# A bidirectional encoder layer: x read once, its squares summed by column, and a second weight group on normalized rows with fused pairs

## The chip, the cores and the metric

One core of one Trainium2 chip runs the kernel. The metric is the device time of one execution in microseconds (us), the median of several runs. Engines are named as in the profile: PE (TensorE, the matmuls), PEld (its weight loads), DVE (VectorE), ACT (ScalarE), POOL (GpSimd, here only the issue of some transfers), SP (the queue that issues most transfers). PSUM is where matmuls accumulate; SBUF holds the tiles that engines read and write.

## The reference

256 positions of width 4096, one layer, everything in float32. The attention itself (three dilated windows, combined) is left out below; it isn't touched.

```python
def rms_norm(x, g, eps=NORM_EPS):
    y = x * lax.rsqrt(jnp.mean(x * x, axis=-1, keepdims=True) + eps) * g

xn = rms_norm(x, norm_g[l])
h = jnp.einsum('bsd,de->bse', xn, w_in[l])            # (256, 4096) x (4096, 14336)
c_val, c_glu, c_gate, q, k, v, a_gate = jnp.split(h, split_pts, axis=-1)
conv_out = conformer_conv(c_val, c_glu, ...) * silu(c_gate)   # c_val * sigmoid(c_glu), conv of 31 taps, LayerNorm, silu
q, k = rms_norm(q, ...), rms_norm(k, ...)
attn_out = longnet_mixture(q, k, v, rel_bias) * silu(a_gate)
x = x + jnp.einsum('bse,ed->bsd', concatenate([conv_out, attn_out]), w_out[l])
```

## The kernel before

**Groups and pairs.** The 18432 columns of both projections are cut into 18 groups of 1024 columns: 14 for `w_in`, 4 for `w_out`. A group has two halves `e` of 512 columns and, with the two halves `s` of 128 positions, four PSUM banks. The 4096 rows of a weight group are 32 row tiles `k` of 128, taken as 16 pairs of 1 MB. Each value goes to PE as two parts, `h` (a cast to the matmul's type) and `l` (what the cast lost), and a product is three matmuls of 128x512: h by h, l by h, h by l. A pair is so 24 matmuls (`plain`, L1253 and L1255); in the first group 12 for each row tile `k` (`products`, L953 to L956).

**Fused pairs.** `fused` (L1112 to L1114, L1224, L1226) does a pair in seven products, 21 matmuls, of sums of weight blocks and sums of row blocks. Its weight sums are made by DVE and ACT when the pair comes (`split_fused`, L1074 to L1096), its row sums once for each pair number (`block_sums`, in `xsum`). `FUSED[g]` lists the pairs of group g that are done so: none in the first two groups, then 5, 7, 7, 7, 7, 6, later none, and 4, 7, 7, 7 in the output groups: 64.

**The order.** It is written out by the program, engine by engine, in one pass. `Stream.step` splits weights as soon as one of four slots (`W_SLOTS`) is free: a cast on ACT (L1026, L1051) and a subtraction on DVE (L1027, L1057), and then asks SP for the pair three places on. Between products, `pump` hands out other work to DVE and ACT by a count of nanoseconds (`left`) that each matmul refills (`credit`). `split_gens` is a list of steps that turn a row tile into normalized parts `nh`, `nl`.

**The first two groups.** The first group multiplies with `xh`, `xl` (x times g, made by `split_x` three row tiles ahead). Meanwhile x is loaded a second time by rows (`load_x`, eight 512 KB pieces), ACT squares it with a running sum (`square_x`, L277), and near the end `finish_rstd` makes 1/rms in a small 128x2 tile and sends it through DRAM to have it as a row. The second group multiplies with `xh`, `xl` again and applies 1/rms when its PSUM banks are read; in it x is loaded a third time by columns, and `split_xn` makes `nh`, `nl` for the groups after it.

Of the kernel before, what the change touches and what calls it, by code (L numbers as in the profile page):

```python
# [11 lines left out]
F32 = mybir.dt.float32  # L12
# [5 lines left out]
P = 128  # L18
# [25 lines left out]
C4 = 16  # L44
XN_LOAD = {1 + (5 * c + 1) // 2: c for c in range(8)}
XN_SQUARE = {n + 5 + s: (c, s) for n, c in XN_LOAD.items() for s in range(2)}
EVAC_TABLE = {"conv": AF.Sigmoid, "agv": AF.Silu, "gate": AF.Silu}
# [17 lines left out]
SUMS = max(FUSED)  # L65
FUSED += [range(4)] + 3 * [range(7)]
# [66 lines left out]
def layer_kernel(  # L133
# [37 lines left out]
    def rsqrt(src, shape, mul, eps, name, wait=True):  # L171

        n = int(np.prod(shape[1:]))
        tag, bufs = ("rs_small", 6) if n <= 32 else ("rs_big", 5)
        v = sb.tile(shape, F32, tag=tag, bufs=bufs, name=name + "v")
        r = sb.tile(shape, F32, tag=tag, bufs=bufs, name=name + "r")
        t = sb.tile(shape, F32, tag=tag, bufs=bufs, name=name + "t")
# [78 lines left out]

    ss = const.tile([P, 2, 8], F32, name="ss")
    xT, x_chunks = {}, {}

    def load_xT(k0, n, queue):  # L260

        t = t4(f"xT{k0}")
        queue.dma_start(
            t[:, :n, :].rearrange("p a b -> p (a b)"),
            x_cols[:, KT + S * k0 : KT + S * (k0 + n)],
        )
        for i in range(n):
            xT[k0 + i] = t[:, i, :]

    def load_x(c):  # L270
        t = t4(f"x{c}").rearrange("p a b -> p (a b)").rearrange("p (s d) -> p s d", s=2)
        nc.sync.dma_start(t, xs[:, :, 512 * c : 512 * c + 512])
        x_chunks[c] = t

    def square_x(c, s):
        junk = t2(f"junk{c}_{s}")
        nc.scalar.activation(  # L277
            junk, x_chunks[c][:, s, :], AF.Square, accum_out=ss[:, s, c : c + 1]
        )

    def split_x(k):
        h, l = new_split(k, "x")
        src = xT.pop(k)
        nc.scalar.activation(h, src, AF.Copy, scale=g_cols[:, k : k + 1])
        nc.vector.scalar_tensor_tensor(
            l, src, g_cols[:, k : k + 1], h.bitcast(F32), op0=ALU.mult, op1=ALU.subtract
        )
        xh[k], xl[k] = h, l
        spend(480, 500)

    def split_xn(k):

        src = xT[k]
        nc.vector.scalar_tensor_tensor(
            src, src, g_cols[:, k : k + 1], state["rstd_row"], op0=ALU.mult, op1=ALU.mult
        )
# [5 lines left out]
        yield 0, 400  # L302
        nc.vector.tensor_sub(l, src, h.bitcast(F32))
        xnh[k], xnl[k] = h, l
        yield 415
        if k % 2 and k // 2 in SUMS:
            yield from block_sums(
                k // 2, src_of=xT, parts=(xnh, xnl), out=xsum, name="xs",
                small=k // 2 in SUMS[5:],
            )  # L310

    split_gens = deque()

    def split_more():

        for gen in list(split_gens)[:4]:
            cost = next(gen, None)
            if cost is None:
                split_gens.remove(gen)
            else:  # L320
                spend(*(cost if isinstance(cost, tuple) else (cost,)))

    def block_sums(j, src_of, parts, out, name, small=False):
# [31 lines left out]

    def finish_rstd():
        tot = const.tile([P, 2], F32, name="sstot")
        nc.vector.reduce_sum(tot, ss, axis=AX.X)
        r = yield from rsqrt(tot, [P, 2], 1.0 / D, NORM_EPS, "rx", wait=False)
        keep = const.tile([P, 2], F32, name="rstd")  # L360
        nc.vector.tensor_copy(keep, r)
        state["rstd"] = [keep[:, s : s + 1] for s in range(2)]
        flat = tc.dram_tile([2, P], F32, name="rstd_dram")
        for s in range(2):
            nc.sync.dma_start(flat[s, :].rearrange("(p o) -> p o", o=1), keep[:, s : s + 1])
        row = const.tile([P, S], F32, name="rstd_row")
        nc.sync.dma_start(
            row, bass.AP(tensor=flat.tensor, offset=flat.offset, ap=[[0, P], [1, S]])
        )
        state["rstd_row"] = row  # L370

# [215 lines left out]
    def ln_gen():  # L587
        while 3 not in conv_done:
            yield
        pm = yield from channel_mean([cT[cb] for cb in range(4)], "mu")  # L590
        mu = sb.tile([P, S], F32, tag="rs_big", bufs=5, name="mu")
        nc.scalar.copy(mu, pm[:, :S])
# [246 lines left out]
    def more_rows():  # L839
        if split_gens:  # L840
            split_more()
        else:
            pump(PRODUCT)
# [39 lines left out]
    def evacuate_sum(g, e, s, acc):  # L883
# [3 lines left out]
        fused = (g, e) in more_tiles  # L887
        if not fused and s == 0 and (g, e) != (1, 1):
            plain_tiles[(g, e)] = half_tile(g, e)
        tile_, pair = (more_tiles if fused else plain_tiles).get((g, e)) or plain_tiles[(g, 0)]  # L890
        t = pair[:, s, :]
        if fused:
            nc.vector.tensor_add(t, t, acc)
            spend(690)
            if fn != AF.Copy:
                nc.scalar.activation(t, t, fn)
                spend(0, 620)
        elif g == 1 and e == 1:
            tile_, first = plain_tiles[(g, 0)]
            t = first[:, s, :]  # L900
            nc.vector.scalar_tensor_tensor(
                t, acc, state["rstd"][s], t, op0=ALU.mult, op1=ALU.mult
            )
            spend(745)
        else:
            scale = state["rstd"][s] if g == 1 else 1.0
            nc.scalar.activation(t, acc, fn, scale=scale)
            spend(0, 620)
# [56 lines left out]
    class Stream:  # L965
# [159 lines left out]
        def group(self, g):  # L1125
# [16 lines left out]
            for slot, j in enumerate(ORDERS[g]):  # L1142
# [5 lines left out]
                self.more = W_MORE if firsts and slot + 2 >= firsts[0] else 0  # L1148
                if g == 1 and slot % 2 == 0 and slot < n_pairs - 2:
                    load_xT(2 * slot + 4, 4, nc.sync)  # L1150
                if slot == 7 and into:
# [26 lines left out]
                if slot < n_pairs - 1:  # L1178
                    self.plain(u, j, rows, one, slot == 0)
                    if g == 1:  # L1180
                        split_gens.extend(split_xn(k) for k in (2 * j, 2 * j + 1))
                    continue
# [17 lines left out]
                if g == 1:  # L1200
                    split_gens.extend(split_xn(k) for k in (2 * j, 2 * j + 1))

# [113 lines left out]
    xT[0] = first_x[:, KT:]  # L1316
    load_pair(0, (0, 512, 1024, 2048), between=lambda: load_xT(1, 1, nc.sync))
    load_xT(2, 2, nc.sync)
    load_pair(1, (0, 1024, 2048))
    load_xT(4, 4, nc.sync)  # L1320
    load_pair(2)
    load_xT(8, 4, nc.sync)
    nc.scalar.copy(warm, ones[:, 0:1])
# [7 lines left out]
    stream.step()  # L1331
    rstd_steps = None
    for g in range(n_in):
        if g > 0:
            stream.group(g)
            continue
        for k in range(KT):
            n = g * KT + k
            if n == 0:
# [3 lines left out]
                for m in (2, 3):  # L1343
                    split_x(m)
                    stream.step()
                rstd_steps = finish_rstd()
            else:
# [11 lines left out]
                else:  # L1359
                    products(n, 1, 0)  # L1360
                    products(n, 1, 1)
            if n % 4 == 0 and 12 + n < KT:
                load_xT(12 + n, 4, nc.sync)
            if n == KT - 4:
                load_xT(0, 4, nc.sync)
            if n in XN_LOAD:
                load_x(XN_LOAD[n])
            if n in XN_SQUARE:
                square_x(*XN_SQUARE[n])
            if k == KT - 3 and groups[g][0] in EVAC_TABLE:  # L1370
                nc.scalar.activation(warm, ones[:, 0:1], EVAC_TABLE[groups[g][0]])
            if 26 <= n <= 28:
                next(rstd_steps)
            elif n == 29:
                list(rstd_steps)
            pump()
# [66 lines left out]
```

## Time and profile before

| what | value |
|---|---|
| runs of the kernel before | 1565.12, 1565.15, 1566.41 us, median 1565.15 us |
| the profiled execution | 1565.9 us, its span 1564.1 us |
| mean granted TensorE clock in it | 1.000 |
| PE busy | 1559.1 us, 6874 matmul records |
| DVE, ACT busy | 1335.1 us, 971.0 us |
| moved by the DMA engines | 357.22 MB, mean 228 GB/s |

The span goes from the first to the last instruction; the execution's time lies 1.8 us around it. Matmuls are pipelined: a record of 128x512 lasts 390 ns, while the next one starts 227 ns after it. One float32 matmul that is not split into parts shows as two records.

### The profile page before, as it was taken

What the parts mean: (1) busy time and instruction counts of PE and PEld (TensorE: products, weight loads), DVE (VectorE), ACT (ScalarE), POOL (GpSimd) and SP (SyncE); (2) the same over time, 40 slices, a digit from 0 to 9 for tenths busy, and PEclk for the clock granted to TensorE, in tenths of its full rate; (3) what the DMA queues carried; (4) which work ended last, traced back from release to release, by engine and by line L of the source; (5) the groups of instructions that cost most, each with busy time, mean ns of one, the idle gap of its engine ahead of it and who ended that gap; (6) DMA issues with size and microseconds to landing.
All of it is one profiled execution on the core that took longest, in us unless ns stands there. A gap on an engine that the chain in (4) does not pass through costs nothing.

```text
span 1564.1 us, 18620 instructions
## 1 busy us (share of the span) xinstructions
PE 1559.1 (100%) x6874; PEld 1290.6 (83%) x6874; DVE 1335.1 (85%) x1495; ACT 971.0 (62%) x1503; POOL 98.9 (6%) x184
## 2 busy tenths in 40 slices
PE   9999999999999999999999999999999999999999
PEld 7888888888888888888888888888888888888887
DVE  5658898999999999898798898789575888999988
ACT  6755555565556566667776786776557754555453
POOL 0000000000000000001130022021010400000000
PEclk9999999999999999999999999999999999999999
DMA  9768565655656555659686488567674965666663
GB/s 373 293 220 298 189 224 206 226 191 201 233 212 228 199 207 213 216 190 284 219 279 216 174 256 269 194 206 272 220 239 161 282 233 201 239 240 242 223 248 122
DMA packets 64523, 357.22 MB, mean 228 GB/s; under 512 B 9104, under 2 KB 11920, under 8 KB 27824
## 3 DMA queue, kind: packets, MB, share of 16 engines
q1 hardware_dynamic: 54096, 326.38, 59.1%
q0 software_dynamic: 10048, 29.37, 6.3%
q8 instruction: 54, 0.88, 0.2%
q10 hardware_dynamic: 288, 0.28, 0.1%
q14 instruction: 37, 0.30, 0.1%
HBM read 337.09 MB, written 18.91 MB: 228 GB/s over the span
## 4 chain that ended last, share of the span: by engine, by line
PE 99%; DMA 0%; DVE 0%; SPq 0%; ACT 0%; DVEq 0%; issue 0%
PE c L1253 44%; PE c L1255 22%; PE m L1224 6%; PE c L1269 4%; PE m L1226 3%; PE c L1271 2%; PE c L1114 2%; PE c L1112 2%; PE c L1224 2%; PE c L1113 2%; PE acc L956 2%; PE acc L953 2%; PE acc L954 2%; PE m L1114 1%; PE c L1226 1%; PE m L1113 1%
## 5 line engine op out<-in xcount | busy, mean ns | idle before, releaser
L1057 DVE TENSOR_TENSOR wl<-raw,wh 128x2048 fp32r<-128x2048 f32 x208 | 475.7, 2289 | 150.2 <-ACT wh L1051 140.9
L1051 ACT CAST wh<-raw 128x1024 fp32r<-128x1024 f32 x416 | 414.9, 1048 | 222.1 <-PE c L1255 134.7
L1253 PE MATMUL c<-wh,nh 128*128 128x512 f32 x1128 | 439.6, 390 | 0.0
L1255 PE MATMUL c<-wh,nl 128*128 128x512 f32 x1128 | 438.9, 389 | 0.0
L1074 ACT CAST t<-raw 128x1024 fp32r<-128x1024 f32 x128 | 134.9, 1054 | 253.9 <-DVE raw L1083 190.5
L1253 PE MATMUL c<-wl,nh 128*128 128x512 f32 x1128 | 280.5, 391 | 0.0
L1253 PEld LDWEIGHTS c<-wh,nh 128*128 128x128 f32 x1128 | 211.7, 188 | 44.0
L1255 PEld LDWEIGHTS c<-wh,nl 128*128 128x128 f32 x1128 | 211.7, 188 | 44.0
L1253 PEld LDWEIGHTS c<-wl,nh 128*128 128x128 f32 x1128 | 211.8, 188 | 43.9
L1075 DVE TENSOR_TENSOR t<-raw,t 128x1024 fp32r<-128x1024 f32 x128 | 156.2, 1221 | 3.6 <-ACT t L1074 0.3
L508 ACT ACTIVATE cp<-a,wT 128x241 f32<-128x241 f32 (+8 forms) x252 | 105.6, 490 | 6.4 <-DVE cT L537 6.3
L1253 PE MATMUL c<-wh,mh 128*128 128x512 f32 x280 | 109.1, 390 | 0.0
L1255 PE MATMUL c<-wh,ml 128*128 128x512 f32 x280 | 108.9, 389 | 0.0
L546 DVE SCALAR_TENSOR_TENSOR cT<-a,wT,cT 128x255 f32<-128x255 f32 (+7 forms) x228 | 95.1, 473 | 0.5
L1083 DVE TENSOR_TENSOR raw<-raw 128x1024 f32<-128x1024 f32 x64 | 78.4, 1225 | 2.2
L1075 DVE TENSOR_TENSOR b<-raw,b 128x1024 fp32r<-128x1024 f32 x64 | 78.0, 1218 | 0.3
L537 DVE TENSOR_TENSOR cT<-cT,cp 128x964 f32<-128x964 f32 (+8 forms) x63 | 73.8, 1172 | 2.8 <-DVE cT L537 0.5
L1253 PE MATMUL c<-wl,mh 128*128 128x512 f32 x280 | 69.2, 389 | 0.0
L1074 ACT CAST b<-raw 128x1024 fp32r<-128x1024 f32 x64 | 67.0, 1047 | 1.9 <-DMA raw<-in_w_dram 1.2
L1255 PEld LDWEIGHTS c<-wh,ml 128*128 128x128 f32 x280 | 52.6, 188 | 10.9
L1253 PEld LDWEIGHTS c<-wl,mh 128*128 128x128 f32 x280 | 52.6, 188 | 10.9
L1253 PEld LDWEIGHTS c<-wh,mh 128*128 128x128 f32 x280 | 52.6, 188 | 10.9
(343 smaller groups left out, 2275.0 us busy)
## 6 DMA issues: line engine op xcount, KB each, us to landing
raw<-in_w_dram SPq DMA_DIRECT2D x286, 1024.0 KB, 4.9
xT<-in_x_cols_dram SPq DMA_DIRECT2D x15, 512.0 KB, 7.3
x<-in_x_dram SPq DMA_DIRECT2D x8, 512.0 KB, 8.2
xr<-in_x_dram SPq DMA_DIRECT2D x8, 512.0 KB, 6.7
out_dram<-xr SPq DMA_DIRECT2D x15, 256.0 KB, 7.4
T<-bias_dram SPq DMA_DIRECT2D x16, 192.0 KB, 5.6
raw<-in_w_dram SPq DMA_DIRECT2D x3, 512.0 KB, 6.7
turn_qk0d<-turn_qk POOLq DMA_DIRECT2D x2, 512.0 KB, 5.1
```

The lines of the kernel that those rows point to most:

```text
L508: nc.scalar.activation(cp[:, t, lo:hi], a[:, t, lo + sh : hi + sh], AF.Copy, scale=wT[:, 4 * cb + t, k : k + 1],)
L537: nc.vector.tensor_add(c[:, :, lo:hi], c[:, :, lo:hi], cp[:, :, lo:hi])
L546: nc.vector.scalar_tensor_tensor(c[:, t, lo:hi], a[:, t, lo + sh : hi + sh], wT[:, 4 * cb + t, k : k + 1], c[:, t, lo:hi], op0=ALU.mult, o ...
L1051: nc.scalar.copy(h, raw_tiles[u][:, k])
L1057: nc.vector.tensor_sub(l, src, h.bitcast(F32))
L1074: nc.scalar.copy(h, src)
L1075: nc.vector.tensor_sub(l, src, h.bitcast(F32))
L1083: nc.vector.tensor_add(r[:, 0:4:3, :], r[:, 0:3:2, :], twice(r[:, 3, :]))
L1224: nc.tensor.matmul(acc, ah, b, start=begin, stop=end)
L1253: nc.tensor.matmul(acc, a[s][0], b[e], start=begin, stop=False)
L1255: nc.tensor.matmul(acc, a[s][1], b[e], start=False, stop=False)
L1269: nc.tensor.matmul(acc, a[s][0], b[e], start=False, stop=end)
```

## The change

- x is loaded once by columns, in eight tiles of four row tiles each, and kept: 12 to 31 in the first seven steps of the first group (`X_LOAD`).
- `sum_squares` replaces the row loads and `square_x`: in eight steps of the first group ACT squares a 128x1024 tile, DVE adds it to `squares`, then folds that to 128x256. In the step of row tile 14, PE multiplies it with `ones` (the sum over partitions, as a row in all partitions) and, twice, uses a 128x128 half of it as weights for one column of `ones` (the same sum as a column). A 128x258 reciprocal root on DVE and ACT follows, with no pass through DRAM.
- `split_xn` runs from row tile 18 of the first group on, on the kept tiles.
- The second group multiplies with `nh`, `nl`, has no factor at its end, and has three fused pairs (6, 8, 12); the third group has six, the eighth seven: 69 in all.
- `split_more` walks up to 20 row tiles instead of four and stops when DVE's count is used up.

```diff
+X_LOAD = {0: 12, 1: 16, 3: 20, 5: 24, 6: 28}
+X_SQUARE = {4: 4, 5: 0, 6: 8, 7: 12, 8: 16, 9: 20, 10: 24, 11: 28}
+N_SPLIT, N_WAIT = 20, 3
...
-FUSED_IN = range(2, 8)
-N_FUSED = dict(zip(FUSED_IN, (5, 7, 7, 7, 7, 6)))
-FUSED = [(2, 4, 6, 8, 10, 12, 13)[: N_FUSED.get(g, 0)] for g in range(N_IN)]
+FUSED_IN = range(1, 8)
+SUMS = (2, 4, 6, 8, 10, 12, 13)
+FUSED = [SUMS if g in FUSED_IN else () for g in range(N_IN)]
+FUSED[1], FUSED[2] = (6, 8, 12), SUMS[1:]
...
+    def sum_squares():
+        total = t4("squares")
+        for i, k0 in enumerate(X_SQUARE.values()):
+            t = t4(f"sq{k0}") if i else total
+            if k0:
+                nc.scalar.activation(t, x_tiles[k0], AF.Square)
...
+            spend(0, 1055)
+            yield
+            if i:
+                nc.vector.tensor_add(total, total, t)
+                spend(1225)
+        total = flat(total)
+        for n in (512, 256):
+            nc.vector.tensor_add(total[:, :n], total[:, :n], total[:, n : 2 * n])
+            spend(160 + n)
+        yield
+        yield
+        yield from finish_rstd(total[:, :S])
...
-    def split_more():
-        for gen in list(split_gens)[:4]:
+    def split_more(forced=False):
+        for gen in list(split_gens)[: 4 if forced else N_SPLIT]:
+            if left[0] <= 0 and not forced:
+                break
...
+    def finish_rstd(total):
+        pm = side("rms")
+        nc.tensor.matmul(pm[:, :S], ones, total, start=True, stop=True)
+        for i in range(2):
+            nc.tensor.matmul(
+                pm[:, S + i : S + i + 1], total[:, P * i : P * i + P], ones[:, 0:1],
+                start=True, stop=True,
+            )
...
-            if g == 1:
-                rows = xh, xl
...
+            if min(X_SQUARE) <= n < KT - 4:
+                next(square_steps, None)
...
+            if "rstd_row" in state:
+                split_gens.extend(split_xn(m) for m in range(n_xn, n - 1))
+                n_xn = max(n_xn, n - 1)
```

On PE, between the last products of row tile 14's step (L956, L974) and the first of row tile 15, the program before goes straight on:

```order
L956 MATMUL acc_0_0_128<-wh_0_392,xh_388 128x512
L956 MATMUL acc_0_1_129<-wh_0_392,xh_388 128x512
L953 MATMUL acc_0_0_128<-wh_1_418,xh_414 128x512
L954 MATMUL acc_0_0_128<-wh_1_418,xl_415 128x512
L953 MATMUL acc_0_1_129<-wh_1_418,xh_414 128x512
```

In the change the three matmuls on `squares` stand there, in the program's only queue for PE:

```order
L974 MATMUL acc_0_0_126<-wh_0_396,xh_392 128x512
L974 MATMUL acc_0_1_127<-wh_0_396,xh_392 128x512
L383 MATMUL rms<-squares,ones 128x256
L385 MATMUL rms<-ones,squares 128x1 x2
L971 MATMUL acc_0_0_126<-wh_1_418,xh_414 128x512
```

So three matmuls are new there, and every later one stands behind them.

On DVE, in the same part of the first group, the program before splits weights of row tiles 14 and 15 (`wh_0_392`, `wh_1_418`) and x (`xl`):

```order
L1027 TENSOR_TENSOR wh_0_392<-raw_278,wh_0_392 128x1024
L383 TENSOR_TENSOR gqk<-vec_cols 128x1
L285 SCALAR_TENSOR_TENSOR xl_415<-xT_160,first_x,xh_414 128x256
L1027 TENSOR_TENSOR wh_1_418<-raw_278,wh_1_418 128x1024
L285 SCALAR_TENSOR_TENSOR xl_440<-xT_238,first_x,xh_439 128x256
```

In the change (`wh_0_396` and `wh_1_418` are row tiles 14 and 15) an addition of squares stands behind each of them, and the two folds behind the last:

```order
L1045 TENSOR_TENSOR wh_0_396<-raw_281,wh_0_396 128x1024
L289 TENSOR_TENSOR squares<-squares,sq_380 128x1024
L303 SCALAR_TENSOR_TENSOR xl_415<-xT_158,first_x,xh_414 128x256
L1045 TENSOR_TENSOR wh_1_418<-raw_281,wh_1_418 128x1024
L289 TENSOR_TENSOR squares<-squares,sq_402 128x1024
L293 TENSOR_TENSOR squares<-squares 128x512
L293 TENSOR_TENSOR squares<-squares 128x256
L303 SCALAR_TENSOR_TENSOR xl_439<-xT_173,first_x,xh_438 128x256
```

The last fold, which PE's new matmuls read, has moved behind the split of row tile 15.

On DVE, at the end of the second group, between the low parts of pairs 14 and 15 (`wl_1427`, `wl_1464`), the program before has one sum of row blocks and four steps of `split_xn`:

```order
L1057 TENSOR_TENSOR wl_1427<-raw_1294,wh_1412 128x2048
L344 TENSOR_TENSOR xsp_1423<-xs_1389,xsp_1423 128x512
L294 SCALAR_TENSOR_TENSOR xT_1202<-xT_1202,first_x,rstd_row 128x256 x3
L294 SCALAR_TENSOR_TENSOR xT_1290<-xT_1290,first_x,rstd_row 128x256
L1057 TENSOR_TENSOR wl_1464<-raw_1339,wh_1451 128x2048
```

In the change (`wl_1457`, `wl_1506`) the sums of the fused pairs' banks stand there, the last two row tiles, and the first steps of the convolution:

```order
L1075 TENSOR_TENSOR wl_1457<-raw_1353,wh_1452 128x2048
L1304 TENSOR_TENSOR us_1469<-conv_0_1470,m_1_1196 128x512
L1305 TENSOR_TENSOR conv_0_1470<-us_1469,m_1_1197 128x512
L323 TENSOR_TENSOR nl_1317<-xT_285,nh_1316 128x256
L323 TENSOR_TENSOR nl_1320<-xT_285,nh_1319 128x256
L1309 TENSOR_TENSOR conv_1_1471<-m_1_1195,us_1469 128x512
L1310 TENSOR_TENSOR conv_1_1471<-m_1_1195,conv_0_1470 128x512
L550 TENSOR_SCALAR cT_1487<-a_1322,wT,vec_cols 128x256 x4
L572 SCALAR_TENSOR_TENSOR cT_1487<-a_1322,wT,cT_1487 128x255 x2
L1075 TENSOR_TENSOR wl_1506<-raw_1395,wh_1490 128x2048
```

Twelve instructions now stand between the two low parts, where five stood.

## Rows read from the trace of the kernel before

**Rows 1.** The page, parts 1 and 2: busy time of each engine; granted clock.

```profile
PE 1559.1 (100%) x6874; PEld 1290.6 (83%) x6874; DVE 1335.1 (85%) x1495; ACT 971.0 (62%) x1503; POOL 98.9 (6%) x184
...
PEclk9999999999999999999999999999999999999999
```

**Rows 2.** The chain that ended last: shares; one piece (start, us, what).

```profile
PE 99%; DMA 0%; DVE 0%; SPq 0%; ACT 0%; DVEq 0%; issue 0%
...
97.79 2.04 PE c L1253 x9
```

**Rows 3.** Waits of PE (total us, times, longest), the only line.

```profile
PE spin L1326 <- DVE ones L169: 1.1, 1, 1.1
```

**Rows 4.** Groups by form, PE: one matmul of each fused input pair.

```profile
L1112 PE MATMUL c<-b,nh 128*128 128x512 f32 x39 | 15.2, 389 | 0.0
```

**Rows 5.** Timeline of PE around the mean's matmul with `ones` (start, us).

```profile
1084.90 0.40 PE L1255 MATMUL c<-wh,nl 128*128 128x512 f32 x1
1085.14 0.60 PE L581 MATMUL mupm<-mutot,ones 128*128 128x256 f32 x2
1085.38 1.28 PE L1253 MATMUL c<-wl,nh 128*128 128x512 f32 x4
```

**Rows 6.** Timeline of PE, unsplit float32 matmuls of the attention.

```profile
741.13 3.61 PE L717 MATMUL psc<-qk,near_q 128*128 128x256 f32 x16
```

**Rows 7.** Groups by form, PEld: weight loads, mean ns.

```profile
L1253 PEld LDWEIGHTS c<-wh,nh 128*128 128x128 f32 x1128 | 211.7, 188 | 44.0
```

**Rows 8.** Timeline of ACT in the first group, row tiles 12 and 13.

```profile
32.55 1.05 ACT L1026 CAST wh<-raw 128x1024 fp32r<-128x1024 f32 x1 [1.26 <-PE acc L956]
33.50 0.63 ACT L277 ACTIVATE junk<-x 128x512 f32<-128x512 f32 x1
...
35.27 1.05 ACT L1026 CAST wh<-raw 128x1024 fp32r<-128x1024 f32 x1 [0.65 <-PE acc L956]
```

**Rows 9.** Groups by form, ACT: the squares of the later LayerNorm.

```profile
L605 ACT ACTIVATE sq<-cT 128x1024 f32<-128x1024 f32 x4 | 3.9, 1048 | 0.0
```

**Rows 10.** Timeline of DVE where one instruction follows another, first and second group.

```profile
21.45 1.22 DVE L1027 TENSOR_TENSOR wh<-raw,wh 128x1024 fp32r<-128x1024 f32 x1
22.59 0.48 DVE L285 SCALAR_TENSOR_TENSOR xl<-xT,first_x,xh 128x256 fp32r<-128x256 f32 x1
...
96.00 2.25 DVE L1057 TENSOR_TENSOR wl<-raw,wh 128x2048 fp32r<-128x2048 f32 x1
98.17 0.70 DVE L437 STREAM_TRANSPOSE turn_a<-conv 128x512 f32<-128x512 f32 x1
```

**Rows 11.** Groups by form, DVE: busy us, mean ns, idle before.

```profile
L1057 DVE TENSOR_TENSOR wl<-raw,wh 128x2048 fp32r<-128x2048 f32 x208 | 475.7, 2289 | 150.2 <-ACT wh L1051 140.9 <-issue 4.7 <-PE c L1253 2.2
...
L1083 DVE TENSOR_TENSOR raw<-raw 128x1024 f32<-128x1024 f32 x64 | 78.4, 1225 | 2.2
...
L1095 DVE TENSOR_TENSOR raw<-raw 128x512 f32<-128x512 f32 x64 | 44.3, 692 | 2.2
...
L546 DVE SCALAR_TENSOR_TENSOR cT<-a,wT,cT 128x255 f32<-128x255 f32 x32 | 13.5, 477 | 0.0
...
L303 DVE TENSOR_TENSOR nl<-xT,nh 128x256 fp32r<-128x256 f32 x32 | 12.5, 418 | 0.0
...
L524 DVE TENSOR_SCALAR cT<-a,wT,vec_cols 128x256 f32<-128x256 f32 x16 | 5.5, 405 | 0.0
...
L187 DVE RECIPROCAL rcr<-rcr 128x256 f32<-128x256 f32 x1 | 1.7, 1744 | 0.0
```

**Rows 12.** Busy time by stretch, the first two groups: PE, PEld, DVE, ACT, POOL, clock.

```profile
0.00:180.00 180.00, 178.78 (x786) 147.58 (x787) 120.78 (x173) 108.54 (x172) 3.07 (x9) 1.00 0.78 284
```

**Rows 13.** Timeline of SP: the issue of a 512 KB piece of x.

```profile
27.09 0.43 SPq L272 DMA_DIRECT2D x<-in_x_dram  x1
```

**Rows 14.** DMA issues by tile: count, KB each, median us to landing.

```profile
x<-in_x_dram SPq DMA_DIRECT2D x8, 512.0 KB, 8.2
```

More of the change, by code (lines that the diff above doesn't have):

```diff
@@ L174, in rsqrt @@
         tag, bufs = ("rs_small", 6) if n <= 32 else ("rs_big", 5)
-        v = sb.tile(shape, F32, tag=tag, bufs=bufs, name=name + "v")
-        r = sb.tile(shape, F32, tag=tag, bufs=bufs, name=name + "r")
-        t = sb.tile(shape, F32, tag=tag, bufs=bufs, name=name + "t")
+        width = [P, S + 2] if tag == "rs_big" else shape
+        v, r, t = (
+            sb.tile(width, F32, tag=tag, bufs=bufs, name=name + i)[:, : shape[1]] for i in "vrt"
+        )
         cost = 160 + n
@@ L255, in new_split, with load_xT @@
         return h, l
[L257 to L262, printed above, removed]
+    xT = {}
+    def load_xT(k0, n, queue, tile_=None, at=0):
+        t = t4(f"xT{k0}") if tile_ is None else tile_
         queue.dma_start(
-            t[:, :n, :].rearrange("p a b -> p (a b)"),
+            t[:, at : at + n, :].rearrange("p a b -> p (a b)"),
             x_cols[:, KT + S * k0 : KT + S * (k0 + n)],
@@ L302, in split_xn @@
         yield 0, 400
+        for _ in range(N_WAIT):
+            yield 0
         nc.vector.tensor_sub(l, src, h.bitcast(F32))
@@ L305, in split_xn @@
         yield 415
[L306 to L310, printed above, removed]
+        if k % 2 and k // 2 in FUSED[FUSED_IN[0]]:
+            yield from x_sums(k // 2)
     split_gens = deque()
-    def split_more():
-        for gen in list(split_gens)[:4]:
+    def split_more(forced=False):
+        for gen in list(split_gens)[: 4 if forced else N_SPLIT]:
+            if left[0] <= 0 and not forced:
+                break
             cost = next(gen, None)
@@ L321, in split_more, with x_sums @@
                 spend(*(cost if isinstance(cost, tuple) else (cost,)))
+    def x_sums(j):
+        yield from block_sums(
+            j, src_of=xT, parts=(xnh, xnl), out=xsum, name="xs", small=j in SUMS[5:]
+        )
     def block_sums(j, src_of, parts, out, name, small=False):
@@ L354, in by_block @@
         return ap.rearrange("p (s a i) -> p s a i", s=2, a=4) if len(ap.shape) == 2 else ap
[L356 to L370, printed above, removed]
+    def finish_rstd(total):
[5 more added lines that the diff above has]
+                start=True, stop=True,
+            )
+        yield
+        steps = rsqrt(pm[:, : S + 2], [P, S + 2], CW / D, NORM_EPS, "rx", wait=False)
+        cost = next(steps)
+        state["held"] -= 1
+        yield cost
+        r = yield from steps
+        state["rstd_row"] = r[:, :S]
+        state["rstd"] = [r[:, S + i : S + i + 1] for i in range(2)]
     gqk = const.tile([P, 1], F32, name="gqk")
@@ L590, in ln_gen @@
         pm = yield from channel_mean([cT[cb] for cb in range(4)], "mu")
-        mu = sb.tile([P, S], F32, tag="rs_big", bufs=5, name="mu")
+        mu = sb.tile([P, S + 2], F32, tag="rs_big", bufs=5, name="mu")[:, :S]
         nc.scalar.copy(mu, pm[:, :S])
@@ L887, in evacuate_sum @@
         fused = (g, e) in more_tiles
-        if not fused and s == 0 and (g, e) != (1, 1):
+        if not fused and s == 0:
             plain_tiles[(g, e)] = half_tile(g, e)
-        tile_, pair = (more_tiles if fused else plain_tiles).get((g, e)) or plain_tiles[(g, 0)]
+        tile_, pair = (more_tiles if fused else plain_tiles)[(g, e)]
         t = pair[:, s, :]
@@ L897, in evacuate_sum @@
                 spend(0, 620)
[L898 to L904, printed above, removed]
-        else:
-            scale = state["rstd"][s] if g == 1 else 1.0
-            nc.scalar.activation(t, acc, fn, scale=scale)
+        else:
+            nc.scalar.activation(t, acc, fn)
             spend(0, 620)
@@ L1316, in layer_kernel @@
     xT[0] = first_x[:, KT:]
[L1317 to L1318 removed]
+    x_tiles[0] = t4("xT1")
+    load_pair(0, (0, 512, 1024, 2048), between=lambda: load_xT(1, 1, nc.sync, x_tiles[0]))
+    load_xT(2, 2, nc.sync, x_tiles[0], 1)
     load_pair(1, (0, 1024, 2048))
[L1320 removed]
+    x_tiles[4] = load_xT(4, 4, nc.sync)
     load_pair(2)
[L1322 removed]
+    x_tiles[8] = load_xT(8, 4, nc.sync)
     nc.scalar.copy(warm, ones[:, 0:1])
@@ L1331, in layer_kernel @@
     stream.step()
-    rstd_steps = None
+    square_steps, n_xn = sum_squares(), 0
     for g in range(n_in):
         if g > 0:
+            split_gens.extend(split_xn(m) for m in range(n_xn, KT))
+            n_xn = KT
+            if g == FUSED_IN[1]:
+                split_gens.extend(x_sums(j) for j in (*SUMS[1:], SUMS[0]) if j not in FUSED[1])
             stream.group(g)
```

44 lines of the change are left out of this document (10 added, 34 removed).

## The prediction

> **What bounds the kernel now.** I read the page first: PE is busy for 1559.1 of 1564.1 us, DVE for 85% of the span, and the granted clock is at its full level (2.4 GHz) in all forty slices [rows 1]. A busy share alone says little where matmuls overlap, so I went to the chain of work that ended last: 99% of it is PE, nothing worth naming is DVE, ACT or a transfer, and inside it nine matmuls take 2.04 us, 0.2267 us each [rows 2]. Last the waits: PE waits once in the whole trace, 1.1 us before its first matmul [rows 3]. The reader is to see that PE is a queue that never runs dry after the first few microseconds. Two things follow. A matmul taken away is worth 0.2267 us at any place. And whatever the change saves on DVE, ACT, SP or the DMA engines is worth nothing, while anything that makes PE wait even once is added in full.
>
> **What it removes, at no price.** Eight row loads of x, its third load by columns, sixteen squares on ACT, the small root, the way of 1/rms through DRAM and four multiplications by 1/rms go. PE waits for none of them now [rows 3], so their removal is worth 0.
>
> **Fewer matmuls.** The trace has 39 fused pairs in the input groups [rows 4]. The new lists have 3 + 6 + 5 x 7 = 44. Five pairs go from 24 matmuls to 21: 15 x 0.2267 = **-3.40 us**.
>
> **Three new matmuls on PE.** The sum over partitions, 128x256 by `ones`, has a twin in the LayerNorm's mean: it starts at 1085.14, the next product at 1085.38, where that product would have started at 1085.14 without it: 0.24 us. The four products behind last 1.28 us instead of 3 x 0.227 + 0.39 = 1.07: another 0.21 [rows 5]. So **+0.45 us**. The two one-column matmuls have no twin. An unsplit float32 matmul is two passes [rows 5], so there are four. Upper bound: a pass with 256 columns, (3.61 - 0.39) / 15 = 0.215 us each [rows 6], 0.86. Lower bound: 0, if passes of one column hide beside their neighbours. With one column there is little to stream and a whole 128x128 weight load to do, so the nearest row is the weight load, 188 ns [rows 7]: **+0.75 us**. By the Trainium skill (TensorE: Matmul & The Clock Gate, section LDWEIGHTS) a load of 128 columns takes 128 / 1.2 = 107 ns, an estimate by which the four would be 0.43 and the sum 0.32 us lower; the 188 ns of the record need not be the distance of two loads, and no row here has loads without long matmuls between them.
>
> **The sum of squares on ACT and DVE.** Each step of the first group is 12 matmuls, 2.72 us. ACT casts weights when PE frees a slot, 2.72 us apart [rows 8]; 26 products later PE reads them, 5.9 us after the release, some 4.6 us after the cast's end. A square of 128x1024 takes 1.05 us [rows 9] for the 0.63 of one half now, and cast, square and x come to 2.6 us: ACT stays inside the step. DVE has a split, an addition and an x in each: back to back, an instruction costs some 0.08 us less than its record (a 1.22 us split is followed after 1.14, a 2.25 us one after 2.17 [rows 10]), so 1.14 + 1.14 + 0.40 = 2.68 of 2.72 us, just inside. The root over 258 columns adds some 3.9 us (a reciprocal of 1.74 [rows 11], five passes of 0.42) over four steps which then have 1.2 us free each: 4.7. For the whole of the first two groups: DVE is busy 120.8 of 180 us [rows 12]; seven additions and the folds (9.7), the root (3.9) and three fused pairs (6.95 each by their seven instructions of [rows 11], 1.22 x 4 + 0.69 x 3, for 2.29 now: 14) make it 148. So it fits on average, and two places have to be walked.
>
> *Where PE meets the column sum.* The cast of row tile 12 starts at 32.55 [rows 8], that of 15 three steps later at 40.71, ending at 41.76. Behind it stand on DVE the split, the last addition and both folds: 1.14 + 1.22 + 0.69 + 0.42, ready at 45.3, or 45.7 if DVE is up to 0.4 behind. PE comes to `rms` before row tile 15, 26 products after the release: at 46.4. I take a wait of **0** (bounds 0 and 0.5), with 0.7 us to spare.
>
> *The last pair of the second group.* PE frees the slot for the cast of pair 14 with the last product of part `t13` of pair 12; 54 products later, 12.24 us, it reads `wl` of pair 15 for the first time. In between: 0.2 to react and two half casts, until 2.25; then on DVE `wl` of pair 14 (2.17), four sums of banks (two by 0.61, two that wait for their neighbour by 0.69), two `nl` (0.34 each), four starts of the convolution (0.33 each), two taps (0.40 each) and `wl` of pair 15 (2.29): 12.1 us. With the full durations of [rows 11] instead it is 13.0. So PE waits between 0 and 0.8 us; I take **+0.2**. In the kernel before, five short instructions stood there. The covers of DVE's new work are thus 0.7 us at the one place and next to nothing at the other.
>
> *Transfers.* The last piece of x goes out behind a weight pair, at about 27.1 as one does now [rows 13], lands 8.2 us later [rows 14], at 35.3, and ACT squares it after row tile 14's cast, at 39.1. Up to weight pair 8 as many pieces of x go out as before, five, one of them a step earlier; afterwards none. 0.
>
> **Sum.** -3.40 + 0.45 + 0.75 + 0 + 0.2 = -2.0 us. The profiled execution, 1565.9 us (span 1564.1, 1.8 around it), goes to 1563.9. The median of the runs shown is 1565.15, 0.75 below that execution, so the forecast for the median is **1563.2 us**.
>
> **Rivals.**
> 1. *The gain stays nearly whole.* One-column passes hide and nothing waits: -3.40 + 0.45 = -2.95, 1562.2 us. For it: two places with a little room. Against it: no row shows a float32 pass under 0.215 us.
> 2. *DVE is late at the end of the second group by more than I take.* Full durations, and the first pairs behind a queue that is a little late everywhere: 0.8 to 1.5 us, so 1563.8 to 1564.5 us. For it: DVE is a strict queue, and convolution steps stand ahead of the `wl` that PE needs. Against it: the discount of 0.08 us is in every pair of rows that I looked at.
> 3. *Slower: PE stands at `rms`.* It is the one new place where PE's queue waits for a chain of transfer, ACT and DVE, and every product stands behind it. Price: one for one. The kernel is slower than before by 0.2% once that wait is over 3.1 + 2.0 = 5.1 us, which is the column sum 5.8 us later than walked, or the last piece of x landing at about 39.1 + 5.8 = 44.9, nearly 18 us after its issue instead of 8.2. Beyond it, at a wait of 7 us, 1570 us. For it: the DMA engines are 78% busy in this stretch [rows 12]. Against it: that landing time is twice the median of its kind.
> 4. *The change doesn't do what it says*: normalized rows are not ready when the second group begins, PE waits for each pair, and fused pairs gain nothing. Both rows of the second group's first pair stand on DVE right behind the weights of row tile 29, which are some 4.6 us and three steps of 2.72 us ahead of PE, so DVE would have to be over 10 us late. With fused pairs as slow as plain ones and one such wait of 5 us, 1563.2 + 3.4 + 5 = 1571.6 us.
>
> **How the numbers follow.** Forecast with its own range 1562.6 to 1563.7: 0.60. Rival 1: 0.12. Rival 2: 0.20. Rivals 3 and 4: 0.08. The range leaves out less than 2 in 10: low 1561.8 (rival 1 less half of a run's scatter), high 1565.0 (rival 2 and the same). A measurement can tell about 0.2%, 3.1 us, from no change; three runs of before lie 1.3 us apart. The forecast, -0.12%, is inside. Faster by over 0.2%, under 1562.0: 0.10, from rival 1 with the scatter of the runs. Within: 0.83. Slower: 0.07, from rivals 3 and 4.
>
> **What would show it.** PE with 15 product records fewer; `rms` twice plus four one-column records, and the distance from the product before them to the second behind; PE's waits still one line (a line for `rms` or `wl` of the second group is a stall, and its length the price); DVE over 140 us in the first two groups. Wrong if PE waits anywhere for more than 1 us, or if the one-column passes cost more than a pass of 256 columns.

## The result, and the profile after

The changed kernel takes 1568.42 us (median of 15 runs, 1564.47 to 1570.80) beside 1565.53 us before (15 runs, 1565.12 to 1566.41): ratio 1.0016, 95% interval 1.0008 to 1.0023 (the ratios here are estimated from all the runs; that of the two medians can differ, here it is 1.0018). That is inside the 0.2% that I called no change, but on the other side of it, and 3.4 us above the upper end of my range. The scatter has changed as well: 1.3 us before, 6.3 us now. The profiled execution took 1566.23 us (span 1564.4), so it is one of the shorter ones.

The page of the changed kernel, parts 1, 2 and 4, which answers to [rows 1, 2]:

```profile
PE 1557.9 (100%) x6865; PEld 1289.1 (82%) x6865; DVE 1374.0 (88%) x1543; ACT 973.6 (62%) x1485; POOL 99.1 (6%) x184
...
PEclk9999999999999999999999999999999999999999
...
PE 89%; issue 6%; DMA 4%; POOL 0%; ACT 0%; SPq 0%; DVE 0%; DVEq 0%; POOLq 0%
```

PE has 9 records fewer: 15 products fewer, six passes of the rms products more, as forecast. But the chain that ended last, 99% PE before, now holds 6% issue (time in which the engine waited for nothing that the profile shows) and 4% DMA. PE's waits say where it was cut (total us, times, longest); before there was only the spin line [rows 3]:

```profile
PE po L788 <- DMA pr<-turn_p6d: 1.4, 1, 1.4
PE spin L1337 <- DVE ones L172: 1.1, 1, 1.1
```

The new wait is not in the groups that the change edits. It is at 980 us, at the attention product of head 6 (`po`, line 788). Timeline of PE there (start, us):

```profile
979.41 1.02 PE L788 MATMUL po<-pr,agv 128*128 128x256 f32 x4
981.87 1.10 PE L788 MATMUL po<-pr,agv 128*128 128x256 f32 x4 [1.44 <-DMA pr<-turn_p6d]
```

Head 5's four passes are followed by 1.4 us of nothing. What was late is in the chain that ended last, the piece of it up to that product (start, us, what):

```profile
954.80 0.01 POOLq L430
954.81 4.82 DMA turn_ag1d<-turn_ag
959.63 1.06 issue
960.70 1.39 POOL agv L437 x3
...
964.07 0.01 POOLq L437
964.08 10.08 DMA turn_p7d<-T
974.17 0.30 issue
974.46 7.27 DMA pr<-turn_p6d
981.74 0.14 issue
981.87 1.10 PE po L788 x4
```

Read it from the end. The last quarter of head 6's transposed probabilities (`pr<-turn_p6d`) went out at 974.46 and landed 7.27 us later. It went out so late because POOL's queue issues in order and, by the rows below, an issue there also waits until the transfer eight places ahead in that queue has landed: here the store of head 7 (`turn_p7d`), which took 10.08 us.

Timeline of POOL, which issues these transfers, in the kernel before and then in the changed one, from the first store of a probability on:

```profile
942.30 0.56 POOL L404 DMA_DIRECT2D turn_p5d<-T  x1 [7.24 <-DVE T L751]
942.85 0.57 POOL L404 DMA_DIRECT2D turn_p6d<-T  x1
956.23 0.54 POOL L404 DMA_DIRECT2D turn_ag1d<-turn_ag  x1 [12.81 <-DVE turn_ag L437]
956.85 2.20 POOL L411 DMA_DIRECT2D pr<-turn_p5d  x4
959.06 1.63 POOL L411 DMA_DIRECT2D pr<-turn_p6d  x3
962.97 0.55 POOL L411 DMA_DIRECT2D pr<-turn_p6d  x1 [2.29 <-DMA pr<-turn_p5d]
963.51 0.56 POOL L404 DMA_DIRECT2D turn_p7d<-T  x1
964.07 2.21 POOL L411 DMA_DIRECT2D agv<-turn_ag1d  x4
```

```profile
954.81 0.56 POOL L430 DMA_DIRECT2D turn_ag1d<-turn_ag  x1 [14.99 <-DVE turn_ag L463]
955.36 0.57 POOL L430 DMA_DIRECT2D turn_p5d<-T  x1
959.09 0.54 POOL L430 DMA_DIRECT2D turn_p6d<-T  x1 [3.16 <-DVE T L777]
960.70 2.32 POOL L437 DMA_DIRECT2D agv<-turn_ag1d  x4 [1.06 <-issue]
964.08 0.56 POOL L430 DMA_DIRECT2D turn_p7d<-T  x1 [1.07 <-DVE cT L550]
...
967.91 0.55 POOL L437 DMA_DIRECT2D pr<-turn_p5d  x1 [2.18 <-DMA turn_p6d<-T]
...
974.46 0.56 POOL L437 DMA_DIRECT2D pr<-turn_p6d  x1 [0.46 <-DMA turn_p7d<-T]
```

Before, heads 5 and 6 were stored at 942 us, ahead of `turn_ag1d`, and their pieces were under way by 963. Now both stand behind `turn_ag1d`, head 6 is stored at 959.09, and five other transfers (four pieces of `agv`, the store of head 7) come ahead of all the pieces of the probabilities. Head 6 is stored 16 us later, and that isn't POOL's doing: the store waits 3.16 us for DVE's transpose `T` (L777), which starts at 958.09 where in the kernel before the transposes of heads 5 and 6 start at 941.03. Its product is only some 8 us later. In the kernel before it is the last four of these twelve passes of PE, at 972.8:

```profile
971.04 2.75 PE L762 MATMUL po<-pr,agv 128*128 128x256 f32 x12
```

So head 6's last piece went out 9.8 us ahead of its product; in the changed kernel the product could have started at about 980.4, 5.9 us behind the issue of a piece that needed 7.27.

The places where the prediction looked are as it wanted them. Timeline of PE around the rms products, and busy time of the first two groups (columns as in [rows 12]):

```profile
46.48 0.59 PE L383 MATMUL rms<-squares,ones 128*128 128x256 f32 x2
46.91 0.50 PE L385 MATMUL rms<-ones,squares 128*128 128x1 f32 x4
47.27 0.49 PE L971 MATMUL acc<-wh,xh 128*128 128x512 f32 x1
47.59 0.40 PE L972 MATMUL acc<-wh,xl 128*128 128x512 f32 x1
```

```profile
0.00:180.00 180.00, 178.86 (x787) 148.26 (x788) 153.49 (x219) 110.84 (x159) 3.07 (x9) 1.00 0.65 236
```

No wait before `rms`, which starts at 46.48 (I had said 46.4). The three new matmuls take 47.59 - 46.48 - 0.23 = 0.89 us, not 1.20. DVE is busy 153 of 180 us (148 worked out), and no line of PE's waits names `wl` of the second group.

### The profile page after: what moved, and what is told of

Its sections match the earlier page's. It is cut to its first block, busy times and chain, and to the rows that moved or that the text cites. A ratio compares the mean times of both kernels' runs of the same rounds, so it can differ in the third digit from the quotient of the medians.

```text
span 1564.4 us, 18607 instructions
## 1 busy us (share of the span) xinstructions
PE 1557.9 (100%) x6865; PEld 1289.1 (82%) x6865; DVE 1374.0 (88%) x1543; ACT 973.6 (62%) x1485; POOL 99.1 (6%) x184
## 4 chain that ended last, share of the span: by engine, by line
PE 89%; issue 6%; DMA 4%; POOL 0%; ACT 0%; SPq 0%; DVE 0%; DVEq 0%; POOLq 0%
PE c L1263 38%; PE c L1265 19%; PE m L1234 6%; PE c L1279 3%; PE m L1236 3%; PE c L1234 2%; PE c L1132 2%; PE c L1130 2%; PE c L1131 2%; PE acc L971 2%; PE acc L972 2%; PE acc L974 2%; PE c L1281 2%; PE c L1236 1%; PE m L1130 1%
## 5 line engine op out<-in xcount | busy, mean ns | idle before, releaser
L1263 PE MATMUL c<-wh,nh 128*128 128x512 f32 x1208 | 470.9, 390 | 0.0
L1265 PE MATMUL c<-wh,nl 128*128 128x512 f32 x1208 | 470.1, 389 | 0.0
L1263 PE MATMUL c<-wl,nh 128*128 128x512 f32 x1208 | 300.5, 391 | 0.0
L1263 PEld LDWEIGHTS c<-wh,nh 128*128 128x128 f32 x1208 | 226.8, 188 | 47.3
L1265 PEld LDWEIGHTS c<-wh,nl 128*128 128x128 f32 x1208 | 226.7, 188 | 47.2
L1263 PEld LDWEIGHTS c<-wl,nh 128*128 128x128 f32 x1208 | 226.8, 188 | 47.0
L534 ACT ACTIVATE cp<-a,wT 128x241 f32<-128x241 f32 (+9 forms) x248 | 103.5, 489 | 4.7 <-DVE cT L563 4.7
L572 DVE SCALAR_TENSOR_TENSOR cT<-a,wT,cT 128x255 f32<-128x255 f32 (+8 forms) x232 | 96.6, 474 | 0.6
L563 DVE TENSOR_TENSOR cT<-cT,cp 128x964 f32<-128x964 f32 (+9 forms) x62 | 72.7, 1173 | 1.9
L1234 PE MATMUL m<-t,xsp 128*128 128x512 f32 x186 | 62.3, 389 | 0.0
```

The lines of the kernel that those rows point to most:

```text
L534: nc.scalar.activation(cp[:, t, lo:hi], a[:, t, lo + sh : hi + sh], AF.Copy, scale=wT[:, 4 * cb + t, k : k + 1],)
L563: nc.vector.tensor_add(c[:, :, lo:hi], c[:, :, lo:hi], cp[:, :, lo:hi])
L572: nc.vector.scalar_tensor_tensor(c[:, t, lo:hi], a[:, t, lo + sh : hi + sh], wT[:, 4 * cb + t, k : k + 1], c[:, t, lo:hi], op0=ALU.mult, o ...
L1234: nc.tensor.matmul(acc, ah, b, start=begin, stop=end)
L1263: nc.tensor.matmul(acc, a[s][0], b[e], start=begin, stop=False)
L1265: nc.tensor.matmul(acc, a[s][1], b[e], start=False, stop=False)
```

## The experiments

Theory A: the change is worth what its products say, less the wait at the attention products (at head 6 in the trace above), whose length hangs on when transfers land; hence the scatter. Rival B: the loss lies in the edited groups (fused pairs, rms products, DVE). The runs come in three sets, each on another chip and beside fresh runs of the kernel before: 27 of them, median 1566.17, in the first set; 25, 1565.59, in the second; 29, 1565.61, in the third.

**after_again** and **after_third**: the changed kernel without an edit, in the first and the third set.

> The changed kernel unedited, on the chip of the runs beside it. Theory A (TensorE stands at the attention product of head 6, because the transposed probabilities come back from DRAM too late behind other transfers in POOL's queue; the length of the wait hangs on when transfers land): the median stays 1 to 4 us above the kernel before, single runs scatter by 3 us or more, the wait of PE for pr<-turn_p6d is there again and is between 1 and 5 us. Rival B (the cost sits in the first two groups, in the fused pairs or in the rms products, which are the same in every run): the runs lie within 1.5 us of each other, and the wait of PE explains less than half of the distance to 1563.2 us.

> The changed kernel unedited once more, beside the three that follow. Theory A: the fastest runs lie at 1563.7 to 1564.5 us, some lie 2 us or more above them, wherever the median comes to stand (1564 to 1568.5 us); the wait for pr<-turn_p6d is there in the profiled run if it is a long one.

Measured: 1564.32 us (1563.94 to 1569.61, 11 runs), ratio 0.9994 (0.9985 to 1.0003); then 1566.38 us (1564.00 to 1569.64, 11 runs), 1.0004 (0.9995 to 1.0012). More than 2 us above their own fastest lie 3 and 6 of 11 runs; in the result above it was 10 of 15; of the kernel before one run in each set. So the same program is 0.06% faster or 0.16% slower than before, by how many of its runs are long. Why that share differs stays open: the sets differ in the chip, and nothing here separates that from chance. Rival B's constant cost is out: the fastest runs are 1.2 to 1.4 us below the fastest of before in these two sets, 0.65 in the result above.

Both profiled executions were long ones (span 1567.8). after_again waits 3.0 us at head 6; after_third waits at two heads:

```profile
PE po L788 <- DMA pr<-turn_p7d: 2.5, 1, 2.5
PE po L788 <- DMA pr<-turn_p6d: 1.0, 1, 1.0
```

Busy time by stretch of after_again around the wait (columns: us; PE, PEld, DVE, ACT, POOL busy; granted clock; DMA share; GB/s), and its timeline of PE ahead of the wait and behind it:

```profile
980.00:985.00 5.00, 2.04 (x10) 1.45 (x9) 1.02 (x3) 3.48 (x6) 0.17 (x1) 0.96 1.04 281
985.00:990.00 5.00, 5.00 (x17) 3.99 (x16) 3.04 (x3) 1.66 (x4) 0.00 (x0) 0.70 0.31 90
```

```profile
974.24 1.98 PE L1263 MATMUL c<-wl,nh 128*128 128x512 f32 x8
...
983.66 1.11 PE L788 MATMUL po<-pr,agv 128*128 128x256 f32 x4 [2.96 <-DMA pr<-turn_p6d]
984.41 3.76 PE L1263 MATMUL c<-wl,nh 128*128 128x512 f32 x8
```

The eight products behind the wait take 3.76 us; such a group of eight takes 1.98 us at 974.24, ahead of it. The granted clock of the stretch from 985 to 990 is 0.70, part of it at the lower of the two levels, 1.2 GHz, and PE had stood for 3 us just before. On these eight products alone 1.8 us are lost beyond the wait.

**late_heads** and **late_heads_again**: the products of heads 5, 6 and 7 are issued later, nothing else moves up to there. Behind them the steps of heads 8 to 11 move a little too.

```diff
         yield from through_dram([tmp], [pr], 128, f"turn_p{h}")
+        if hg == 1:
+            end = now[0] + 4000
+            while now[0] < end:
+                yield
```

> The attention products of heads 5, 6 and 7 are issued 24 products of TensorE (5.4 us) later; nothing else moves up to there and POOL's queue has the same order. Theory A: the wait for pr<-turn_p6d is gone, PE's list of waits has the spin line alone, the span of the profiled run is 1562.2 to 1562.9 us, the median 1563.3 to 1564.6 us, the runs scatter by 1.5 us at most as those of the kernel before, ratio to before 0.9985 to 0.9994. Rival B: nothing changes, median 1567 us or more and ratio 1.001 to 1.002.

> As late_heads: median 1563.7 to 1564.8 us, no run above 1566 us, ratio to before 0.9983 to 0.9995. Rival: runs of 1567 us or more here too, so that the wait at head 6 is not what makes the long runs.

Measured: 1564.50 us (1563.84 to 1565.52), ratio 0.9991 (0.9982 to 1.0000), span 1563.2, 0.3 above what was expected, with one new wait, 0.3 us for ACT at a sum of weights (L1238); then 1564.20 us (1563.79 to 1564.65), 0.9990 (0.9981 to 0.9999), span 1562.5. No run of 22 is more than 2 us above the fastest, where the unedited kernel has 9 of 22. The waits of PE in late_heads_again:

```profile
PE spin L1341 <- DVE ones L172: 1.1, 1, 1.1
```

POOL issues head 6's last piece at 974.58 there, no earlier than the 974.46 of the changed kernel; only its reader comes later. So it is the waits at these products, heads 6 and 7, that make the long runs, and without them the change gains 1.4 to 1.7 us by the medians.

**ag1_on_sp**: the four pieces of `agv<-turn_ag1d` leave POOL's queue.

```diff
-        from_dram(ds, dsts, n)
+        from_dram(ds, dsts, n, nc.sync if name == "turn_ag1" else None)
```

> Order of TensorE, VectorE and ScalarE as in the changed kernel; only the four pieces of agv<-turn_ag1d (heads 4 to 7) are issued by SP and no longer stand in POOL's queue ahead of the probabilities of heads 5, 6 and 7. Theory A1 (the order of POOL's queue makes head 6 late: each issue also waits for landings of earlier transfers): the pieces of pr<-turn_p6d are issued by about 968.5 us (last one at 974.5 in the changed kernel), the wait of PE at head 6 is gone, no run is more than 1.7 us above the fastest, median 1563.9 to 1565. Rival A2 (head 6 is late because its probabilities are computed and transposed late, at 958.1 us, and two trips of 7 to 8 us each follow, whatever stands in the queue; or because the memory is full there, DMA share 1.0): the wait is still there in some runs, which reach 1567 us or more. SP's weights may come up to 7 us later around 960 us, which would show as a wait for wh or wl.

Measured: 1564.10 us (1563.74 to 1568.37, 11 runs), ratio 0.9990 (0.9982 to 0.9999). PE does not wait in the profiled execution. Timeline of POOL:

```profile
964.30 2.20 POOL L437 DMA_DIRECT2D pr<-turn_p5d  x4
966.69 1.63 POOL L437 DMA_DIRECT2D pr<-turn_p6d  x3 [0.19 <-ACT cp L534]
970.37 0.55 POOL L437 DMA_DIRECT2D pr<-turn_p6d  x1 [2.05 <-DMA turn_p7d<-T]
```

Head 6's last piece goes out at 970.37 instead of 974.46 with TensorE, VectorE and ScalarE in the same order. So the order of POOL's queue holds head 6 back by 4.1 us (A1), and in this trace that is enough to end the wait. But the piece still waits for head 7's store, at 970.37 and not by 968.5 as I wrote: the late transpose and store of head 6 (A2) stay as they were, and of the 11.5 us by which the piece is later than before this edit gives back only these 4.1. One run of 11 reached 1568.37, which I had ruled out; no trace shows why, and one run of before in this set reached 1567.72.

**late_and_sp**: both edits.

> Both edits, the later attention products of late_heads and the pieces of agv<-turn_ag1d on SP: the landing of head 6 has 5.4 us more before its product and fewer transfers ahead of it. Theory A: no wait of PE behind the first group, no run above 1565.5 us, median 1563.7 to 1564.5 us. If SP's later weights cost something, the median is above that of late_heads_again.

Measured: 1564.15 us (1563.68 to 1564.66, 11 runs), ratio 0.9990 (0.9981 to 0.9999), PE's waits the spin line alone. As late_heads_again; SP's four issues cost nothing that shows.

**before_early_head7** and **before_early_head7_more**: such a wait made in the kernel before, where it was not. The planned return of heads 4 to 7 is cut by 4000 ns in the one, by 7000 ns in the other; up to there only head 7's product, and DVE's read of it, changes its place.

```diff
-        yield from through_dram([tmp], [pr], 128, f"turn_p{h}")
+        ds = to_dram([tmp], 128, f"turn_p{h}")
+        yield from landing()
+        from_dram(ds, [pr], 128)
+        end = now[0] + (LANDING - 4000 if hg == 1 else LANDING)
+        while now[0] < end:
+            yield
```

> The kernel before, with the attention product of head 7 issued 26 positions (3.6 us of products that stood ahead of it) earlier, and no other change. Its last piece was issued at 973.5 us in the trace of before and such pieces land 6.3 us after their issue (median), so at 979.8 us, and the product would now stand at 979.1 us. Theory A: PE shows a new wait for pr<-turn_p7d of 0.5 to 2.5 us, the median rises by 0.5 to 3 us, and the runs scatter more than the 1.3 us of the kernel before. Rival B (such a wait costs nothing measurable, or PE makes it up): median within 0.4 us of the kernel before, scatter as before.

> The kernel before with the attention product of head 7 right behind that of head 6, 40 products earlier than in before, so at about 973.7 us, 6 us or more ahead of the landing of its last piece (979.8 us worked out). Theory A with the clock: PE waits 4 to 8 us for pr<-turn_p7d in every run; behind it some 9 products stand 0.427 us apart (1.2 GHz) as they do behind the wait of 3.3 us in a run of the changed kernel, for 1.5 to 2 us more; median 1571 to 1576 us, above 1566.2 by the wait and these 2 us. Rival (what the wait costs is made up behind it, or only the wait counts): no products at 0.427 us, and the median up by the wait alone.

Measured: the first 1566.20 us (1565.36 to 1572.25, 11 runs), ratio 1.0009 (1.0000 to 1.0018): the median did not move and the profiled execution shows no wait, where I had expected one of 0.5 to 2.5 us and a median 0.5 to 3 us higher. In that execution the pieces of head 7 landed in 4.8 us (median), not in the 6.3 of before that I had counted on. But 3 of 11 runs lie 4.4 us or more above the fastest, at 1569.84, 1570.15 and 1572.25. That is the scatter of the changed kernel, made in the kernel before by moving the product of one head. The second 1573.35 us (1572.13 to 1576.38, 4 runs), 1.0052 (1.0036 to 1.0067). Waits of PE, and busy time around it:

```profile
PE po L767 <- DMA pr<-turn_p7d: 5.0, 1, 5.0
```

```profile
975.00:980.00 5.00, 1.53 (x5) 1.29 (x5) 0.54 (x2) 0.00 (x0) 0.00 (x0) 0.56 0.93 308
980.00:985.00 5.00, 5.00 (x18) 3.95 (x17) 1.21 (x3) 0.00 (x0) 0.00 (x0) 0.76 0.00 0
```

With this wait of 5.0 us (and one of 0.2 in the first group) the span is 1570.8, 6.7 us longer than the 1564.1 of before: 1.5 to 1.7 us more than the waits, as Theory A with the clock had it.

**old_pairs** and **old_pairs_mended**: the fused pairs of the kernel before with all else of the change. In old_pairs the product of value and gate of the second group is left out, and pair 2, whose sums are made last, was the first that needs its sums.

```diff
-FUSED[1], FUSED[2] = (6, 8, 12), SUMS[1:]
+FUSED[1], FUSED[2], FUSED[7] = (), (2, 4, 6, 8, 10), SUMS[:6]
```

```diff
-FUSED[1], FUSED[2] = (6, 8, 12), SUMS[1:]
+FUSED[1], FUSED[2], FUSED[7] = (), (4, 6, 8, 10, 12), SUMS[:6]
...
-        if k % 2 and k // 2 in FUSED[FUSED_IN[0]]:
+        if k % 2 and k // 2 in (6, 8, 12):
```

> The changed kernel with the 39 plus 25 fused pairs of the kernel before in place of 44 plus 25: 15 more products, everything else of the change kept (columns of x kept, squares, rms products, normalized rows in the second group). In its order the attention products of heads 4 to 7 stand after the planned trips of all of them. Theory A: no wait for pr<-turn_p6d; against the kernel before only the rms products (0.9 us) and nothing else remain: median 1566.0 to 1567.2 us, scatter 1.5 us. Rival B (the fused pairs, not the wait, cost the time): the median is at or below that of the kernel before.

> As old_pairs, 15 more products than the changed kernel, with the sums of pairs 6, 8 and 12 made in the second group as in the changed kernel and pair 4 the first fused pair of the third group, so that no sum is needed before it is made, and with the product of value and gate in the second group done behind both evacuations. Theory A: everything but the pairs is as in the changed kernel, so the time is that of late_heads plus 15 x 0.2267 = 3.4 us: median 1567.2 to 1568.5 us unless a new wait of PE shows, which then is to be subtracted. Rival B (the fused pairs give less than their products): median below 1566.7.

Measured: old_pairs 1580.65 us (1580.44 to 1581.11, 4 runs), 13 us or more above what was expected. It tells nothing of the pairs, since my edit made a wait of its own; of waits it tells more:

```profile
PE c L1130 <- ACT xsp L366: 10.7, 1, 10.7
```

old_pairs_mended 1567.12 us (1566.86 to 1567.86, 11 runs), ratio 1.0008 (0.9999 to 1.0017); its one new wait is 0.4 us for ACT in the first group. That is 3.02 us above ag1_on_sp of the same set, 0.4 less than 15 products, 0.8 less if that wait is in its other runs too. And with the pairs back the wait at the heads is gone. Its order is not that of before: POOL stores head 5 at 948.37, ahead of `turn_ag1d`, but head 6 only at 968.79, with its product moved along. So it is the new pairs, or what goes with them, that move the heads into the order in which PE waits. Through which of their effects (the second group without taps of the convolution, the heads' first products later, sums at other places) was not separated, and this edit moves a product of value and gate besides.

**five_columns**: the one-column products five times each.

```diff
-        for i in range(2):
+        for i in 5 * (0, 1):
```

> The two one-column products behind the 128x256 product of the rms tile are issued five times each, ten products, 16 passes more. As the prediction priced them (188 ns a pass) they take 3.0 us more; by the trace of the changed kernel (0.11 us between passes) 1.8 us more. TensorE's stretch from the first rms pass to the next product is 0.79 us in the changed kernel: 2.6 us by the trace, 3.8 us by the prediction. The median is above that of late_heads by the same, or by more where head 6 makes PE wait.

Measured, the timeline of PE:

```profile
46.26 0.59 PE L383 MATMUL rms<-squares,ones 128*128 128x256 f32 x2
46.69 2.29 PE L385 MATMUL rms<-ones,squares 128*128 128x1 f32 x20
48.84 0.49 PE L971 MATMUL acc<-wh,xh 128*128 128x512 f32 x1
```

From the first pass to the next product 2.58 us instead of 0.79: 16 passes take 1.79 us, 0.112 us each, not 0.188. The time is 1569.21 us (1567.11 to 1572.58, 8 runs); the fastest is 3.4 us above that of ag1_on_sp, more than the 1.79 of the passes, and the profiled execution waits twice, for heads 7 (1.4 us) and 6 (1.3 us). The granted clock stayed at 1.00 behind these two.

**longer_landing**: every trip through DRAM is planned 2 us longer.

```diff
-LANDING = 8500
+LANDING = 10500
```

> The changed kernel with the planned time of every trip through DRAM at 10.5 us in place of 8.5; the attention product of head 6 comes 32 products (7.3 us) later than in the changed kernel, and every later step that waits for a trip moves too. Theory A: no wait for pr<-turn_p6d, no long runs, median 1563.7 to 1564.8 us, unless one of the moved steps makes a new wait, which the list of PE's waits then names.

Measured: 1571.08 us (1568.69 to 1572.06, 7 runs), ratio 1.0031 (1.0020 to 1.0042). Against what I expected, the slowest of the repairs. Its waits of PE:

```profile
PE po L788 <- DMA pr<-turn_p5d: 2.9, 1, 2.9
PE po L788 <- DMA pr<-turn_p4d: 1.3, 1, 1.3
...
PE c L1279 <- DVE wl L1075: 0.6, 1, 0.6
```

The wait for head 6 is gone, but now the store of head 4 stands behind `turn_ag1d` too (954.50), and heads 4 and 5 are late. More planned time did not help: it moved the order of POOL's queue again. The 4000 ns of late_heads, put where they move only the products, did.

## Why the prediction was wrong

**The step that failed** is *Transfers*, priced at 0, and with it "PE's waits still one line". The sentence that they rest on, "whatever the change saves on DVE, ACT, SP or the DMA engines is worth nothing", is right for the work removed. But I took it also for work that is moved, and looked only at transfers of the first group. What the runs show in its place: some 800 us behind the second group DVE transposes head 6's probabilities 16 us later, POOL's queue has another order, and PE waits 1.4 us there in the profiled execution, 3.0 us in after_again, 2.5 and 1.0 in after_third. With the products issued later (late_heads) the waits and the long runs are gone; with the pairs of before (old_pairs_mended) too. How much room the attention's transfers had I never read. It was in the trace of before: 9.8 us from the issue of head 6's last piece to its product, against landings of 5.3 to 7.9 us for the stores and pieces of heads 5 to 7. In the changed kernel 5.9 us are left. The prediction's own sign of being wrong, "PE waits anywhere for more than 1 us", came true, at a place that it hadn't walked.

**The size of a wait.** Rival 3 priced one at "one for one". In the traces a wait costs more than it is listed with. Against the span of one trace without it (late_heads_again 1562.5 for the changed kernel, 1564.1 for before, 1565.1 for old_pairs_mended) a listed wait of 1.4 us cost 1.9 with the clock at 1.00; 3.0 us cost 5.3, as did 2.5 and 1.0 close together in after_third; 5.0 cost 6.7; old_pairs' 11.0 (10.7 and 0.3) cost 13.6. These differences are uncertain by some 0.5 us: the spans of late_heads, late_heads_again and ag1_on_sp are 1563.2, 1562.5 and 1562.3, and waits of 0.2 to 0.4 us in the first group stand in some traces and not in others. At and behind the longer waits the granted clock fell to between 0.50 and 0.76 of full speed in a stretch of 5 us.

**Fewer matmuls, -3.40 us**: the count was right. Some of the gain is given back: in the same 540 us from 150 to 690 PE does 2380 matmuls before, 2378 in old_pairs_mended, 2377 in the changed kernel and 2376 in late_heads_again, so three or four are lost, 0.7 to 0.9 us. Matmuls on the sums of pairs 12 and 13 have records of 392 to 399 ns, most of them 394 or 395, against 389 on other sums, and start 232 or 233 ns apart where others start 227; the new lists hold more of them. Why they are slower was not tested.

**Three new matmuls, +1.20 us**: measured 0.89. The term mis-sized is the one-column passes: 0.112 us each, so 0.45 and not 0.75. The row I took, the weight load's 188 ns, is no distance between loads. By the Trainium skill (TensorE: Matmul & The Clock Gate, section LDWEIGHTS) a load of P columns takes about P / 1.2 ns, so 107 ns for 128, an estimate by which this term would have been 0.43; the measured 0.112 us a pass lies 5 ns above it.

**Wait at `rms`, 0**: right. **Wait at the last pair of the second group, +0.2**: no wait is listed there, so 0 in place of 0.2. **Removals, 0**: nothing in the runs speaks against it.

**The sum after the fact**: -3.40 + 0.89 + 0.9 = -1.6 us without the wait. The two runs of late_heads measure -1.7 and -1.4 by their medians. So the forecast of -2.0 comes near for the work. With the 1.9 of the wait it is +0.3, as the profiled execution went from 1565.9 to 1566.23; that agrees by construction, since the 1.9 is itself a difference of spans. The median of the changed kernel, 1568.42, is some 4 us above those of late_heads: most of its runs are longer than the one that was profiled, and that they wait like the two long executions is inferred from late_heads, not seen in each.

## What to carry to other kernels

Where the order of work comes out of planned times, an edit early in the program changes the order in every queue behind it: compare the order of the DMA queues over the whole program, and wherever a product reads a transfer, set its room against how long such transfers take around there. When single runs scatter more than before, look for a wait that hangs on a landing. A queue that issues in order and waits for earlier landings passes one late transfer on to all behind it; it helped here to give the reader more room or to move other transfers to another queue, not to plan all trips longer.

## What was not expected of the hardware

- A short stand of TensorE cost more than its length in some of these traces: behind 3.0 us of waiting eight products took 3.76 us instead of 1.98, at the lower clock level; behind 1.4 us, and behind 1.4 and 1.3 us in one stretch, the granted clock stayed at 1.00.
- The stores and pieces of the probabilities of heads 5 to 7 landed in 5.3 to 7.9 us in the kernel before. In the changed kernel the store of head 7 took 10.08 us and the pieces of head 5 a median of 10.3. The DMA share from 960 to 980 us is 0.96 to 1.05 in both, so it doesn't tell them apart; why they took longer was not tested.
